# A transformer block stack in split fp32: one more chunk of the feed-forward nets by seven block products, with partial sums kept in PSUM

## The chip, the cores and the metric

The kernel runs on one core of a Trainium2 chip. A core has TensorE (PE, matmuls; its weight loads are listed apart as PEld), VectorE (DVE), ScalarE (ACT), GpSimd (POOL) and SyncE (SP), each with its own row of instructions, and 16 DMA engines. The metric is the time of one execution on the device in microseconds (us), as the median of several runs; a profile of one execution shows what each engine did.

## The reference

Two layers, each of four parts with a layer norm behind each: a feed-forward net `ffn1`, a mixer, cross attention, and a second feed-forward net `ffn2`. The sequence has 256 tokens, the model is 1024 wide, the nets are 2816 wide inside. All of it is fp32.

```python
def swiglu(x, w_gate, w_up, w_down):
    return (jax.nn.silu(x @ w_gate) * (x @ w_up)) @ w_down
...
    for l in range(DEPTH):
        h = layer_norm(ALPHA * h + 0.5 * swiglu(h, ffn1_gate[l], ffn1_up[l], ffn1_down[l]), ln_g[l, 0], ln_b[l, 0])
        ...  # mixer (convolution, recurrence, pooling) and cross attention, each with its layer norm
        h = layer_norm(ALPHA * h + 0.5 * swiglu(h, ffn2_gate[l], ffn2_up[l], ffn2_down[l]), ln_g[l, 3], ln_b[l, 3])
```

The change is in the four nets (`swiglu`) alone.

## The kernel before

**A product is three matmuls.** Each fp32 operand is split in two parts that PE multiplies at its quick fp32 rate: `split` has ACT round a block into `whi` (line 75) and DVE subtract that from the block to give `wlo` (line 76). `mm_rows` then issues hi x hi, hi x lo and lo x hi into one PSUM bank; all its matmuls carry line 132. Every weight of the model is so cast once on ACT and subtracted once on DVE, in pieces of 128x1024. There are eight `whi` and eight `wlo` buffers, used in turn, so ACT and DVE can be at most eight pieces ahead of PE. Blocks come in from DRAM into `raw` buffers (six, in turn) and a few named ones (`spare0` to `spare2`, `lng`, `lnb`) through SP's queue.

**A net.** `ffn` walks over the 2816 hidden columns in five chunks of 512 (numbers 0 to 4) and one of 256 (number 5). A chunk makes its gate and up products for both tiles of 128 tokens in PSUM banks with the tag `acc` (four in turn), applies silu and the product of the two (`activate`, `gated`), turns the result by DMAs and DVE transposes (`turn`, the tiles `dealt` and `square`), splits it into `ah` and `al`, and leaves it in `acts`. The down projection adds up in four banks with the tag `dn`; `both(c, u)` is one slab of it: two splits and 24 matmuls, 128x512. `todo` lists eight slabs of chunks 0 to 3, and they are put between the products of later chunks so that PE has work while a chunk is being turned. `later[c]` tells how many stand right after chunk c.

**Two ways to make a chunk.** `hidden` loads gate and up in eight pieces and issues 96 matmuls of 128x512. `by_seven` takes x as 2 token tiles by 2 halves of the depth, and the weights as 2 halves of the depth by (gate, up), and makes the 2 by 2 block product with seven block products in place of eight: 7 x 12 = 84 matmuls. The sums of blocks of x (`bx`) are made once per net after chunk 1; those of the weights are made in each chunk, in place: `parts_of(r, plus)` adds one block to another on DVE (line 702) and splits the sum, and `more` (line 738) has POOL issue a DMA that adds a block from DRAM into one that has been loaded by `block` (line 685) and used. Which buffers a chunk's blocks live in goes round by `homes`. The first and last blocks are

```python
w00 = block(gate, 0, pieces(*homes[0]))
w01 = block(up, 0, pieces(*homes[1]))
w10 = block(gate, 1, pieces(*homes[3]))
```

and `w11` is loaded after the third product. The seven products are combined partly in PSUM (`run(..., True)` adds to a bank that already holds something) and partly in SBUF: `taken` (line 734) is ACT's copy of a bank, `put` (line 721) is one DVE operation on a bank and an SBUF half. `s` (`sg`) is the gate half, `e` and `f` are the two token tiles of the up half (`halves`, in chunk 5 all of them are in `both`). The tail of a chunk is handed out as functions: `left()` applies the last silu and the last put, what it returns multiplies gate and up (`gate_all`, line 779) and starts the turn, and what that returns ends the turn. So the caller can have the next chunk's instructions written ahead of a tail.

`sevens = (2, 4) if early is not None else (2, 4, 5)` says which chunks go that way; `early` is set in the first net of the program only. So "the last three nets" are ffn2 of layer 0, ffn1 of layer 1 and ffn2 of layer 1; below they are nets 2, 3 and 4. Chunk 5 in them is a half-wide `by_seven` with one piece per block.

**What sets the order.** The tile framework orders the instructions of each engine as they are written, apart from groups under `issue_after`, which are held until a named instruction has been written out, and it puts in the semaphores. Each engine then works off its own row in that order. So an instruction that waits holds up everything behind it on its engine.

## Time and profile before

| | before |
|---|---|
| time, median of 3 runs | 1062.99 us (1062.97 to 1064.28) |
| span of the profiled execution | 1061.1 us |
| PE busy | 1051.2 us, 99%, 6014 matmuls |
| DVE busy | 933.2 us, 88%, 1246 instructions |
| ACT busy | 662.0 us, 62%, 909 |
| POOL busy | 94.7 us, 9%, 128 |
| granted PE clock | 9 tenths or more in all 40 slices |
| moved by DMA | 251.06 MB, mean 237 GB/s |

The span is from the first to the last instruction of one execution that was recorded; no other time of that execution is given, and the median of the timed runs lies 1.9 us above its span. Busy times overlap between engines. PE's matmuls are pipelined, so its duration per matmul (some 0.38 us for 128x512) is longer than the step from one to the next. "L76" is line 76 of the kernel. In a timeline row, the bracket at the end is the idle time of the engine just before the group and what ended it. The chain is the work that ended last, followed back from the end.

### The profile page before, as it was taken

The page shows a single profiled execution, that of the slowest core. Times are in us where ns is not written, and L with a number is a line of the kernel's source. Part 1 is how long each engine was busy: PE and PEld are TensorE (multiplying, and loading weights), DVE is VectorE, ACT ScalarE, POOL GpSimd, SP SyncE. Part 2 cuts the span into 40 slices and gives each one's busy share as a digit, 9 for nine tenths or more (in the row PEclk, how much of TensorE's full clock was granted, in tenths as well). Part 3 has the DMA queues.
Part 4 walks back from the last instruction along what each step waited for, and adds up shares of the span by engine and source line. Part 5 has one row for each costly group of instructions (what it writes and reads, how often), then busy time and mean ns, then how long its engine had stood idle before and what let it go on. Part 6 is the DMA issues. An engine that isn't in the chain of part 4 may idle for free.

```text
span 1061.1 us, 16496 instructions
## 1 busy us (share of the span) xinstructions
PE 1051.2 (99%) x6014; PEld 934.8 (88%) x6014; DVE 933.2 (88%) x1246; ACT 662.0 (62%) x909; POOL 94.7 (9%) x128
## 2 busy tenths in 40 slices
PE   9999999999999999999999999999999999999996
PEld 7888888889899888889888888998998998888896
DVE  6998898989988789887898987999899787898787
ACT  6675775676557566655665656666774655675661
POOL 8002001000000001010001001010000000000001
PEclk9999999999999999999999999999999999999999
DMA  9999984854675589988789978866636675799971
GB/s 364 296 320 280 260 272 146 268 166 155 210 271 179 171 281 231 363 192 217 239 305 254 338 224 208 271 233 222 206 122 215 241 243 162 242 303 294 241 194 68
DMA packets 142306, 251.06 MB, mean 237 GB/s; under 512 B 11249, under 2 KB 51985, under 8 KB 142225
## 3 DMA queue, kind: packets, MB, share of 16 engines
q1 hardware_dynamic: 130656, 228.89, 65.0%
q0 software_dynamic: 10992, 19.94, 10.9%
q10 hardware_dynamic: 576, 1.18, 0.3%
q8 instruction: 47, 0.77, 0.3%
q14 instruction: 35, 0.28, 0.1%
HBM read 234.50 MB, written 1.05 MB: 222 GB/s over the span
## 4 chain that ended last, share of the span: by engine, by line
PE 92%; DVE 3%; DMA 2%; issue 2%; ACT 1%; POOL 0%; DVEq 0%; ACTq 0%; POOLq 0%
PE acc L132 61%; PE dn L132 27%; DVE wlo L76 2%; PE acc L199 1%; DMA raw<-in_ffn_gate_dram 1%; DMA raw<-in_ffn_down_dram 1%; ACT whi L75 0%; PE dn L1139 0%; DVE raw L702 0%; PE dn L1213 0%; DMA lng<-in_ln_g_dram 0%; DMA h<-in_x_dram 0%; DVE al L76 0%; PE acc L581 0%; DVE square L531 0%
## 5 line engine op out<-in xcount | busy, mean ns | idle before, releaser
L75 ACT CAST whi<-raw 128x1024 fp32r<-128x1024 f32 (+1 forms) x452 | 456.1, 1042 | 201.2 <-PE dn L132 58.0
L76 DVE TENSOR_TENSOR wlo<-raw,whi 128x1024 fp32r<-128x1024 f32 (+1 forms) x452 | 534.5, 1211 | 53.1 <-ACT whi L75 47.1
L132 PE MATMUL acc<-whi,xT 128*128 128x512 f32 (+1 forms) x1064 | 313.9, 372 | 0.0
L132 PEld LDWEIGHTS acc<-whi,xT 128*128 128x128 f32 x1064 | 199.0, 189 | 26.9 <-DVE xT L76 0.3
L132 PE MATMUL acc<-wlo,xT 128*128 128x512 f32 (+1 forms) x532 | 197.9, 372 | 0.0
L132 PE MATMUL dn<-whi,ah 128*128 128x512 f32 x346 | 131.5, 380 | 0.0
L132 PE MATMUL dn<-wlo,ah 128*128 128x512 f32 x346 | 131.3, 379 | 0.0
L132 PE MATMUL dn<-whi,al 128*128 128x512 f32 x346 | 131.1, 379 | 0.0
L132 PE MATMUL acc<-xT,whi 128*128 128x512 f32 x480 | 117.6, 381 | 0.0
L132 PEld LDWEIGHTS acc<-wlo,xT 128*128 128x128 f32 x532 | 100.6, 189 | 13.4
L132 PEld LDWEIGHTS acc<-xT,whi 128*128 128x128 f32 x480 | 86.8, 190 | 9.8
L132 PE MATMUL dn<-whi,xT 128*128 128x512 f32 x288 | 87.7, 380 | 0.0
L132 PEld LDWEIGHTS dn<-wlo,ah 128*128 128x128 f32 x346 | 65.4, 189 | 9.6 <-DVE wlo L76 0.6
L132 PEld LDWEIGHTS dn<-whi,al 128*128 128x128 f32 x346 | 65.4, 189 | 9.2
L132 PEld LDWEIGHTS dn<-whi,ah 128*128 128x128 f32 x346 | 65.4, 189 | 9.0
L132 PEld LDWEIGHTS acc<-xT,wlo 128*128 128x128 f32 x480 | 62.9, 191 | 3.2
L132 PE MATMUL acc<-xT,wlo 128*128 128x256 f32 x480 | 63.2, 275 | 0.0
L132 PE MATMUL acc<-wlo,kTh 128*128 128x512 f32 (+1 forms) x176 | 61.7, 351 | 0.0
L132 PE MATMUL acc<-whi,kTl 128*128 128x512 f32 (+1 forms) x176 | 61.7, 351 | 0.0
L132 PE MATMUL acc<-whi,kTh 128*128 128x512 f32 (+1 forms) x176 | 61.7, 351 | 0.0
L132 PEld LDWEIGHTS dn<-whi,xT 128*128 128x128 f32 x288 | 54.4, 189 | 7.6
L132 PE MATMUL dn<-wlo,xT 128*128 128x512 f32 x144 | 54.6, 379 | 0.0
(252 smaller groups left out, 1296.8 us busy)
## 6 DMA issues: line engine op xcount, KB each, us to landing
raw<-in_ffn_up_dram SPq DMA_DIRECT2D x88, 512.0 KB, 5.7
raw<-in_ffn_down_dram SPq DMA_DIRECT2D x88, 512.0 KB, 5.6
raw<-in_ffn_gate_dram SPq DMA_DIRECT2D x84, 512.0 KB, 5.6
raw<-in_w_in_dram SPq DMA_DIRECT2D x48, 512.0 KB, 4.8
dealt<-sg SPq DMA_DIRECT2D x80, 128.0 KB, 4.5
raw<-in_ffn_up_dram POOLq DMA_DIRECT2D x19, 512.0 KB, 6.3
raw<-in_ffn_gate_dram POOLq DMA_DIRECT2D x16, 512.0 KB, 9.4
raw<-in_ca_k_dram SPq DMA_DIRECT2D x16, 512.0 KB, 5.2
```

The lines of the kernel that those rows point to most:

```text
L75: rounded = nc.scalar.copy(hi, src)
L76: lows.append(nc.vector.tensor_tensor(lo, src, hi.bitcast(F32), op=ALU.subtract))
L132: turns.append(nc.tensor.matmul(o, w, x, start=start, stop=stop, skip_group_check=more))
L199: turns.append(nc.tensor.transpose(pt[:, k, :], src[:, (4 * j + k) * P : (4 * j + k + 1) * P], unit))
```

## The change

In the last three nets `sevens` becomes (2, 3, 4, 5): chunk 3 is made by seven block products as well, and the two slabs that stood behind chunk 3 (`later[3] = 2`; the 2 for chunk 5 was not used) go between the products of chunk 3, as `between[0]` and `between[1]`, as chunks 2 and 4 have them. Chunks 2 to 5 then follow each other by seven. Since chunk 3 now takes a place in `sevens`, the tuple of `homes` goes on by one for chunk 4.

In all four nets the sums of the seven products are kept in PSUM for longer. The bank of the first product, `o`, is copied to a second bank, `total`, by ACT, and the third product adds into `o`, which silu then reads directly; products 4, 5 and 7 add into `total`, and after the fourth ACT writes `-total` into a fourth bank, `less`, to which product 6 adds. That takes away two `put` per chunk (one for `s`, one for `e`) and the copy of `f`. The `put` for `f` now reads `total` itself, before product 7 adds to it.

Last, `left()` is called through to the turn at once in every chunk but chunk 4 (before: in every chunk whose successor is not in `sevens`).

```diff
@@ -718,7 +718,7 @@
                         mm_rows(o, x[0][:, k, :], x[1][:, k, :], wh, wl, k == 0 and not more, k == 3, more)
 
                 def put(o, a, op, b):
-                    nc.vector.tensor_tensor(ordered(o), in_order(a), ordered(b), op=op)
+                    nc.vector.tensor_tensor(ordered(o), ordered(a), in_order(b), op=op)
 
                 if ncol == CHUNK:
                     s, ef = activations(), fp.tile([P, NT, CHUNK], F32, tag="up", name="halves", bufs=1)
@@ -737,43 +737,39 @@
                     for i, x in enumerate(to):
                         nc.gpsimd.dma_start(x, part_of(m, j, i), accum_op=ALU.add)
 
-                o = [bank() for _ in range(3)]
-                run(o[0], part_of_x(0, 0), parts_of(w00))
-                taken(s[:, 0, :], o[0])
-                run(o[1], bx[0], parts_of(w00, w01))
+                o, total, one = (bank() for _ in range(3))
+                run(o, part_of_x(0, 0), parts_of(w00))
+                nc.scalar.copy(total, o)
+                run(one, bx[0], parts_of(w00, w01))
+                taken(e, one)
                 more(w01, up, 1)
-                run(o[2], part_of_x(0, 1), parts_of(w10))
+                run(o, part_of_x(0, 1), parts_of(w10), True)
                 between[0]()
-                put(s[:, 0, :], o[2], ALU.add, s[:, 0, :])
+                activate(s, 0, o)
                 w11 = block(up, 1, pieces(*homes[2]))
-                run(o[0], bx[1], parts_of(w00, w11), True)
+                run(total, bx[1], parts_of(w00, w11), True)
                 if ncol == CHUNK:
                     more(w00, gate, 1)
-                copied = taken(e, o[0])
+                less = bank()
+                copied = nc.scalar.mul(less, total, -1.0)
                 between[1]()
-                nc.scalar.activation(s[:, 0, :], s[:, 0, :], AF.Silu)
-                put(e, o[1], ALU.subtract, e)
                 if ncol == CHUNK:
-                    run(o[0], bx[2], parts_of(w01), True)
-                    taken(f, o[0])
-                    o.append(bank())
-                    run(o[3], bx[3], parts_of(w11))
-                    put(f, o[1], ALU.subtract, f)
-                    run(o[0], part_of_x(1, 1), parts_of(w00), True)
+                    run(total, bx[2], parts_of(w01), True)
+                    put(f, e, ALU.subtract, total)
+                    run(less, bx[3], parts_of(w11), True)
+                    run(total, part_of_x(1, 1), parts_of(w00), True)
                 else:
-                    o.append(bank())
-                    run(o[3], bx[3], parts_of(w11))
-                    run(o[0], bx[2], parts_of(w01), True)
-                    taken(f, o[0])
-                    put(f, o[1], ALU.subtract, f)
+                    run(less, bx[3], parts_of(w11), True)
+                    run(total, bx[2], parts_of(w01), True)
+                    put(f, e, ALU.subtract, total)
                     with tc.issue_after(copied.ins):
                         w = parts_of(w00, w10)
                     between[2]()
-                    run(o[0], part_of_x(1, 1), w, True)
+                    run(total, part_of_x(1, 1), w, True)
 
                 def left():
-                    act = activate(s, 1, o[0])
-                    put(e, o[3], ALU.add, e)
+                    act = activate(s, 1, total)
+                    put(e, e, ALU.add, less)
 
                     def gate_all():
                         passed.append((act, nc.vector.tensor_tensor(s, s, ef, op=ALU.mult)))
@@ -818,7 +814,7 @@
                 return w, ah[:, 2 * u : 2 * u + 2, :], al[:, 2 * u : 2 * u + 2, :]
 
 
-            sevens = (2, 4) if early is not None else (2, 4, 5)
+            sevens = (2, 4) if early is not None else (2, 3, 4, 5)
             passed, dealts, turn_memory = [], [], None
             bx = []
 
@@ -845,7 +841,7 @@
                             rows_of(a, i, k, m, c == u == k == 0, apart)
 
             todo = [(c, u) for c in range(4) for u in range(2)]
-            later = (0, 0, 0, 2, 0, 2) if early is None else (0, 1, 0, 1, 0, 2)
+            later = (0, 0, 0, 0, 0, 0) if early is None else (0, 1, 0, 1, 0, 2)
             for c, (c0, ncol) in enumerate(chunks):
                 if not c:
                     acts.append(first()())
@@ -881,7 +877,7 @@
                         held = []
                         with tc.issue_after(lows[-1].ins):
                             acts[4] = acts[4](held)
-                    acts.append(left() if c + 1 in sevens else left()() if c == 5 else left()()())
+                    acts.append(left() if c == 4 and 5 in sevens else left()() if c == 5 else left()()())
                     if ncol < CHUNK:
                         with tc.issue_after(passed[-1][0].ins), tc.issue_after(passed[-1][1].ins):
                             held[0]()
```

The next rows are those of DVE at the boundary from chunk 2 to chunk 3 in net 2. Before, raw_4211 and raw_4212 are chunk 2's w00 with the second gate block added, raw_4476 and the raw tiles behind it are chunk 3's plain gate pieces, and halves_4224 is chunk 2's `ef`.

```order
L76 TENSOR_TENSOR wlo_4441<-raw_4211,whi_4440 128x1024
L76 TENSOR_TENSOR wlo_4445<-raw_4212,whi_4444 128x1024
L76 TENSOR_TENSOR wlo_4481<-raw_4476,whi_4480 128x1024
L76 TENSOR_TENSOR wlo_4485<-raw_4477,whi_4484 128x1024
L76 TENSOR_TENSOR wlo_4493<-raw_4488,whi_4492 128x1024
L721 TENSOR_TENSOR halves_4224<-acc_4226,halves_4224 128x512
L76 TENSOR_TENSOR wlo_4497<-raw_4489,whi_4496 128x1024
L76 TENSOR_TENSOR wlo_4557<-raw_4552,whi_4556 128x1024
L721 TENSOR_TENSOR halves_4224<-acc_4418,halves_4224 128x512
L76 TENSOR_TENSOR wlo_4561<-raw_4553,whi_4560 128x1024
```

After, on the same engine at the same place; raw_4207 and raw_4208 are that block of chunk 2, raw_4469 and raw_4470 chunk 3's w00, raw_4473 and raw_4474 its w01, halves_4220 is chunk 2's `ef`, acc_4222 is `total`, acc_4355 is `less`.

```order
L76 TENSOR_TENSOR wlo_4435<-raw_4207,whi_4434 128x1024
L76 TENSOR_TENSOR wlo_4439<-raw_4208,whi_4438 128x1024
L76 TENSOR_TENSOR wlo_4487<-raw_4469,whi_4486 128x1024
L702 TENSOR_TENSOR raw_4469<-raw_4469,raw_4473 128x1024
L76 TENSOR_TENSOR wlo_4491<-raw_4470,whi_4490 128x1024
L721 TENSOR_TENSOR halves_4220<-halves_4220,acc_4222 128x512
L76 TENSOR_TENSOR wlo_4509<-raw_4469,whi_4508 128x1024
L702 TENSOR_TENSOR raw_4470<-raw_4470,raw_4474 128x1024
L721 TENSOR_TENSOR halves_4220<-halves_4220,acc_4355 128x512
L702 TENSOR_TENSOR raw_4469<-raw_4469,raw_4589 128x1024
```

Chunk 3's first splits are now followed by the sums of its blocks (L702), each made from the tile that was just split, and chunk 2's put for `f` stands behind the first two splits of chunk 3, with the adds between.

The second place is DVE in chunk 4 of net 2, from the splits of the fourth product's block, after which POOL's adding DMA for the same block is issued, to the splits for the seventh product, which read what that DMA brought. Before (raw_4712 and raw_4713 are w00; sg_4724 and halves_4725 are the gate half and `ef`):

```order
L76 TENSOR_TENSOR wlo_4837<-raw_4712,whi_4836 128x1024
L76 TENSOR_TENSOR wlo_4842<-raw_4713,whi_4841 128x1024
L76 TENSOR_TENSOR wlo_4865<-raw_4860,whi_4864 128x1024
L76 TENSOR_TENSOR wlo_4869<-raw_4861,whi_4868 128x1024
L76 TENSOR_TENSOR wlo_4899<-raw_4716,whi_4898 128x1024
L721 TENSOR_TENSOR sg_4724<-acc_4728,sg_4724 128x512
L76 TENSOR_TENSOR wlo_4903<-raw_4717,whi_4902 128x1024
L76 TENSOR_TENSOR wlo_4921<-raw_4831,whi_4920 128x1024
L76 TENSOR_TENSOR wlo_4925<-raw_4832,whi_4924 128x1024
L76 TENSOR_TENSOR wlo_4942<-raw_4712,whi_4941 128x1024
L721 TENSOR_TENSOR halves_4725<-acc_4727,halves_4725 128x512
L76 TENSOR_TENSOR wlo_4946<-raw_4713,whi_4945 128x1024
```

After (raw_4731 and raw_4732 are w00, square_4726 and al_4725 the turn of chunk 3):

```order
L76 TENSOR_TENSOR wlo_4857<-raw_4731,whi_4856 128x1024
L76 TENSOR_TENSOR wlo_4862<-raw_4732,whi_4861 128x1024
L531 STREAM_TRANSPOSE square_4726<-dealt_4719 128x4x4x32 x2
L76 TENSOR_TENSOR wlo_4886<-raw_4881,whi_4885 128x1024
L76 TENSOR_TENSOR wlo_4890<-raw_4882,whi_4889 128x1024
L76 TENSOR_TENSOR al_4725<-square_4726,ah_4724 128x1024
L76 TENSOR_TENSOR wlo_4918<-raw_4735,whi_4917 128x1024
L76 TENSOR_TENSOR wlo_4922<-raw_4736,whi_4921 128x1024
L76 TENSOR_TENSOR wlo_4939<-raw_4851,whi_4938 128x1024
L76 TENSOR_TENSOR wlo_4943<-raw_4852,whi_4942 128x1024
L76 TENSOR_TENSOR wlo_4959<-raw_4731,whi_4958 128x1024
L76 TENSOR_TENSOR wlo_4963<-raw_4732,whi_4962 128x1024
```

The two puts have gone from between, and chunk 3's two transposes and its `al` split have come in; the splits of the slab's pieces, of w01 and of w11 stand there in both.

The third place is POOL's row of adding DMAs from chunk 2 to chunk 5 of net 2. Before, with raw_4211, raw_4212 of chunk 2, raw_4712 to raw_4717 of chunk 4 and raw_4965 of chunk 5:

```order
L738 DMA raw_4211<-in_ffn2_gate_dram 128x2x512
L738 DMA raw_4212<-in_ffn2_gate_dram 128x2x512
L738 DMA raw_4716<-in_ffn2_up_dram 128x2x512
L738 DMA raw_4717<-in_ffn2_up_dram 128x2x512
L738 DMA raw_4712<-in_ffn2_gate_dram 128x2x512
L738 DMA raw_4713<-in_ffn2_gate_dram 128x2x512
L738 DMA raw_4965<-in_ffn2_up_dram 128x4x256
```

After:

```order
L738 DMA raw_4207<-in_ffn2_gate_dram 128x2x512
L738 DMA raw_4208<-in_ffn2_gate_dram 128x2x512
L738 DMA raw_4473<-in_ffn2_up_dram 128x2x512
L738 DMA raw_4474<-in_ffn2_up_dram 128x2x512
L738 DMA raw_4469<-in_ffn2_gate_dram 128x2x512
L738 DMA raw_4470<-in_ffn2_gate_dram 128x2x512
L738 DMA raw_4735<-in_ffn2_up_dram 128x2x512
L738 DMA raw_4736<-in_ffn2_up_dram 128x2x512
L738 DMA raw_4731<-in_ffn2_gate_dram 128x2x512
L738 DMA raw_4732<-in_ffn2_gate_dram 128x2x512
L738 DMA raw_4982<-in_ffn2_up_dram 128x4x256
```

Four adding DMAs of 512 KB have come in for chunk 3, between those of chunk 2 and chunk 4.

## The prediction

> **What bounds the kernel now.** I read the page first, then the chain of waits, the stretches of the three nets that change, and the timeline of DVE inside the second net (ffn2 of layer 0). The page and its groups:

> ```profile
> PE 1051.2 (99%) x6014; PEld 934.8 (88%) x6014; DVE 933.2 (88%) x1246; ACT 662.0 (62%) x909; POOL 94.7 (9%) x128
> PE 92%; DVE 3%; DMA 2%; issue 2%; ACT 1%; POOL 0%; DVEq 0%; ACTq 0%; POOLq 0%
> ```

> TensorE (PE) is busy throughout and is 92% of the chain. But VectorE (DVE) has only 12% of the span left, and the chain of waits shows what happens at the end of the second net:

> ```profile
> 372.79 41.44 PE acc L132 x192
> ...
> 519.21 1.15 DVE wlo L76
> ...
> 520.40 7.17 PE dn L132 x32
> ```

> While PE runs alone, 192 matmuls start in 41.44 us, 0.216 us each. At 520.40 the chain comes to PE out of a DVE split: there PE's next weights were late. The stretches from the first split of chunk 2 to the last down weights, one row for each of the last three nets:

> ```profile
> 390.30:520.30 130.00, 130.00 (x643) 114.57 (x641) 113.54 (x116) 80.69 (x92) 12.35 (x11) 1.00 0.89 255
> 557.50:687.50 130.00, 130.00 (x645) 115.00 (x644) 114.78 (x116) 81.09 (x92) 12.36 (x11) 1.00 0.88 257
> 913.00:1044.00 131.00, 131.00 (x650) 115.87 (x649) 114.64 (x118) 79.40 (x90) 12.33 (x11) 1.00 0.84 240
> ```

> Columns are length, then busy time of PE, weight loads, DVE, ACT, POOL, then the granted clock (1.00). DVE's idle time is 16.5, 15.2 and 16.4 us. This is the budget on which the change draws. Most of it came in 14 gaps:

> ```profile
> DVE wlo L76 <- ACT whi L75: 11.2, 10, 2.0
> DVE al L76 <- ACT ah L75: 3.0, 2, 2.4
> DVE square L531 <- DMA dealt<-sg: 1.6, 2, 0.8
> ```

> **The change part by part.** First, what an instruction costs on DVE when it follows another without a gap, from its timeline:

> ```profile
> 394.04 1.31 DVE L531 STREAM_TRANSPOSE square<-dealt 128x512 f32<-128x512 f32 x2 [0.78 <-DMA dealt<-sg]
> 397.70 1.23 DVE L76 TENSOR_TENSOR al<-square,ah 128x1024 fp32r<-128x1024 f32 x1 [2.36 <-ACT ah L75]
> ...
> 411.51 1.22 DVE L702 TENSOR_TENSOR raw<-raw 128x1024 f32<-128x1024 f32 x1
> 413.92 2.36 DVE L76 TENSOR_TENSOR wlo<-raw,whi 128x1024 fp32r<-128x1024 f32 x2 [1.19 <-ACT whi L75]
> ...
> 468.18 6.89 DVE L76 TENSOR_TENSOR wlo<-raw,whi 128x1024 fp32r<-128x1024 f32 x6
> ...
> 493.57 0.68 DVE L721 TENSOR_TENSOR halves<-acc,halves 128x512 f32<-128x512 f32 x1
> 494.17 2.35 DVE L76 TENSOR_TENSOR wlo<-raw,whi 128x1024 fp32r<-128x1024 f32 x2
> ...
> 499.99 0.42 DVE L721 TENSOR_TENSOR both<-acc,both 128x256 f32<-128x256 f32 x1
> 500.32 2.35 DVE L76 TENSOR_TENSOR wlo<-raw,whi 128x1024 fp32r<-128x1024 f32 x2
> ```

> Six 128x1024 splits take 6.89 us, the last one 1.22, so one follows another after (6.89 - 1.22) / 5 = 1.135 us; after a gap it costs 1.22, 0.085 more. The 512-wide one costs 494.17 - 493.57 = 0.60, the 256-wide one 0.33.

> *PE.* Chunk 3 goes from 96 matmuls to 7 x 12 = 84: 12 x 0.216 = 2.6 us less in each of three nets, 7.8 in all. This is the floor: nothing else leaves PE.

> *DVE.* Chunk 3 splits 7 blocks of two pieces instead of 8 pieces (+6), adds +4 block sums (w00+w01, then +w11, two pieces each), and one 128x1024 gate product: 11 x 1.135 = 12.5 us. Its two 512-wide products with PSUM become two put's: 0. The seeded banks take away two put's in chunks 2 and 4 (4 x 0.60) and two in the half chunk 5 (2 x 0.33): -3.1. Sum +9.4 us per net. In the first net only the four put's go (-2.4 us of DVE), in a net that PE sets: 0.

> [...]

> *ACT.* It takes 6 casts more, and as many evictions as before in a seven chunk (5). Its 80.7 us busy in 130 become about 87: hidden, and the cover is large. The seed of total (after product 1, needed by product 4) has products 2, 3 and a slab, 48 x 0.216 = 10.4 us, as cover; the seed of less has a slab and product 5, 7.8 us. If that cover went, each would cost PE some 0.6 us.

> *The new wait.* put(f) now reads the bank that product 7 adds to, so PE's seventh product waits for a DVE instruction (before: for an ACT copy). In DVE's row that put stands behind the next chunk's first splits, so product 7 also waits for the next chunk's first load. Cover: product 6, 2.6 us, and DVE's lead. I price it within DVE's sum: while DVE is the later engine, it is the same lateness.

> *What of the 9.4 fits.* DVE's lost time before is 16.5 + 14 x 0.085 = 17.7 us. If DVE binds to the end of the net, the net changes by 9.4 + (lost time after) - 17.7. Lost time after: (a) the three gaps of the rows above (0.78, 2.36, 1.19) lie ahead of the first moved instruction and stay: 4.3 + 0.3 = 4.6. (b) An add that is followed at once by the split of its own sum costs 1.19 (the row at 413.92: add, cast on ACT, split). The order after has this once more in chunk 3 (raw_4470), once in chunk 5, and once in chunk 5 with a put between: 2 x 1.27 + (1.27 - 0.60) = 3.2. That makes 7.8, and -0.5 for the second net; with the idle budgets of the others +0.7 and -0.4. Sum -0.2 us, if no DMA is late.

> (c) The DMAs that add a block into one already loaded (line 738, `more`). POOL's timeline, where the gate pair of chunk 4 is issued; ACT's, where the cast waits for it; the landings of the whole second net up to 520; and the page's issues, plain (SPq) and adding (POOLq):

> ```profile
> 470.84 2.42 POOL L738 DMA_DIRECT2D raw<-in_ffn_gate_dram  x2 [14.75 <-DVE wlo L76]
> ```

> ```profile
> 481.15 1.05 ACT L75 CAST whi<-raw 128x1024 fp32r<-128x1024 f32 x1 [1.03 <-DMA raw<-in_ffn_gate_dram]
> ...
> 484.81 2.00 ACT L75 CAST whi<-raw 128x1024 fp32r<-128x1024 f32 x2 [2.13 <-DMA raw<-in_ffn_gate_dram]
> ```

> ```profile
> L738 POOL DMA_DIRECT2D raw<-in_ffn_up_dram x5: 1189/1194/1295, 393.6 to 489.8; - x5
> L738 POOL DMA_DIRECT2D raw<-in_ffn_gate_dram x4: 1189/1192/1281, 411.9 to 472.0; - x4
> ...
> DMA to landing us min/median/max: 5.9/9.5/12.8
> ```

> ```profile
> raw<-in_ffn_gate_dram SPq DMA_DIRECT2D x84, 512.0 KB, 5.6
> ...
> raw<-in_ffn_up_dram POOLq DMA_DIRECT2D x19, 512.0 KB, 6.3
> raw<-in_ffn_gate_dram POOLq DMA_DIRECT2D x16, 512.0 KB, 9.4
> ```

> The adding DMAs rise from 9 to 13 per net. Each gate one is issued after the fourth product's split and has to be back before the seventh's. In chunk 4 after the change, 8 big instructions and two transposes lie between on DVE: 8 x 1.135 + 1.3 = 10.4 us, less the cast's 1.05: 9.3. The pair issued at 470.84 landed in time for the casts at 481.15, 10.3 us on, and at 484.81, 12.8 us after the second issue (ACT waited 1.03 and 2.13 for them): 1.0 to 3.5 us of lost time, 0 at the shortest landing. I take 1.0, near the first of the pair, since fewer SP loads run beside it. Chunk 3 has the same cover at the median landing, 0.2; its first load, which may start only after chunk 2's fifth product is split, has 7 instructions (7.9 - 1.05 = 6.9 us) against 5.6: 0, or 2.5 if it is as slow as 9.4. I take 0.4 for both. So (c) is 1.4 per net, between 0 and 7.0.

> Sum: -0.2 + 3 x 1.4 = +4.0 us. The page's execution has a span of 1061.1 us; the median of the runs, 1062.99, lies 1.9 above it, and I carry that over: 1061.1 + 4.0 + 1.9 = 1067.0 us.

> **The rivals.** (1) PE stays the bound and the change gains. The point is 17.7 - 9.4 = 8.3 us of lost time per net: below it the kernel is faster, at 5.7 the full 7.8 us come (1055.2). For it: many casts waited only because DVE was ahead and the ring of eight whi buffers was full:

> ```profile
> L75 ACT CAST whi<-raw 128x1024 fp32r<-128x1024 f32 (+1 forms) x452 | 456.1, 1042 | 201.2 <-PE dn L132 58.0
> ```

> and such waits go when the lead goes. Against it: (a) and (b) alone are 7.8 and are none of this kind, which leaves 0.5 for everything else. But (a) and (b) are taken from single rows, and a third off them already decides it. Chance 0.28.

> (2) No DMA is late: the adding DMAs land as the fast ones here do (5.9), the cover of 9.3 suffices, and gain and cost cancel: 1061.1 - 0.2 + 1.9 = 1062.8. For it: the up ones land after 6.3 at the median. Against: the gate ones took 9.4. Chance 0.25. [...]

> (3) The close pair in chunk 4 lands as late as 12.8 in each net: 3.5 + 0.4 = 3.9 per net, +11.5: 1074.5. For it: the trace has it so in the second net, and more adding DMAs share the queues. Chance 0.14.

> **How the numbers follow.** The forecast (1 to 2 us of late DMA per net, slower by 0.4%) has the remaining 0.33. A measurement of this kernel tells about 0.2%, 2.1 us, from no change. Faster is rival 1: 0.28; the same is rival 2: 0.25; slower are the forecast and rival 3: 0.47. The range goes from 1057.7 (rival 1 with two thirds of its gain, 1063.0 - 5.3; some 0.12 below) to 1074.5 (rival 3 in every net; some 0.07 above).

> **What the new profile would show.** If the steps hold: DVE's busy time in the three stretches rises by 8 to 9 us and its idle falls to about 9 to 10; PE shows waits that it hardly had before, for wlo (L76) late in chunks 4 and 5 and for halves (L721) ahead of seventh products, 2.5 to 5 us per net; chunk 3 on PE is 18.1 us long plus its slabs. The first net keeps its length. Wrong would be: no PE wait over 1 us in these nets (rival 1); waits of DVE for casts that wait for a DMA of 3 us and more (rival 3); or a wait of PE for ACT's seeds, which I price at 0.

## The result and the profile after

The kernel after takes 1078.07 us (median of 4 runs, 1075.05 to 1078.72) against 1063.63 for the kernel before in the same runs: a ratio of 1.0129 [1.0116, 1.0141], 14.4 us slower. The sign was the forecast one; the size, 4.0 us, was far off, and the time lies above the range. The profiled execution after has a span of 1076.5 us and took 1078.4, so it too has 1.9 us around its span.

From the page after, the lines on the engines, on the chain by engine, and the two adding DMA groups:

```profile
PE 1050.8 (98%) x5978; PEld 930.9 (86%) x5978; DVE 956.7 (89%) x1257; ACT 680.4 (63%) x936; POOL 110.0 (10%) x140
...
PE 70%; issue 12%; DMA 8%; DVE 7%; ACT 2%; POOL 1%; DVEq 0%; POOLq 0%; SPq 0%; ACTq 0%
...
raw<-in_ffn_up_dram POOLq DMA_DIRECT2D x25, 512.0 KB, 6.3
raw<-in_ffn_gate_dram POOLq DMA_DIRECT2D x22, 512.0 KB, 9.1
```

36 matmuls have gone, as worked out, and DVE's busy time has grown by 23.5 us. But the chain was 92% PE and is now 70%; DMA and DVE have 15% of it, and the adding DMAs are no slower at the median (9.1 us, before 9.4). What PE waits for in the changed kernel (total us, number of waits, longest; before, its list has two waits, both ahead of the first net):

```profile
PE acc L132 <- DVE halves L721: 13.5, 4, 4.5
PE dn L132 <- ACT whi L75: 2.2, 3, 1.3
...
PE acc L132 <- ACT whi L75: 0.4, 1, 0.4
PE acc L132 <- DVE wlo L76: 0.2, 1, 0.2
```

Four waits carry most of it, and three of the four are one place: the first matmul of product 7 in chunk 4, once in each of the three nets. PE's timeline:

```profile
494.71 0.45 PE L132 MATMUL acc<-whi,xT 128*128 128x512 f32 x1 [3.56 <-DVE halves L721]
...
664.93 0.77 PE L132 MATMUL acc<-whi,xT 128*128 128x512 f32 x1 [4.52 <-DVE halves L721]
...
1029.30 0.76 PE L132 MATMUL acc<-whi,xT 128*128 128x512 f32 x1 [4.01 <-DVE halves L721]
```

Measured from the start of one matmul to the next, these stalls are 3.72, 4.68 and 4.17 us beyond the usual step: 12.6 us. The second and third cost more than their wait. The windows around the second (PE, weight loads, DVE, ACT, POOL, granted clock, DMA share, GB/s), and last the one behind the first stall:

```profile
660.00:665.00 5.00, 0.48 (x3) 0.11 (x2) 4.18 (x4) 2.21 (x3) 0.52 (x1) 0.87 0.74 270
665.00:670.00 5.00, 5.00 (x12) 4.00 (x13) 4.65 (x5) 3.16 (x4) 0.77 (x1) 0.50 0.73 105
...
495.00:500.00 5.00, 5.00 (x35) 4.67 (x34) 4.87 (x5) 3.80 (x6) 0.57 (x1) 1.00 0.80 127
```

Behind the stall of 4.68 us the granted clock is 0.50, and PE issues 12 matmuls in 5 us where 23 would fit; that cost 2.7 us, and 1.5 behind the one of 4.17. Behind 3.72 the clock stayed at 1.00; the last section says what tells the cases apart. Adding up all steps between matmuls that were longer than usual, the three nets waited 1.8, 0.6 and 0.6 us before and 7.1, 9.0 and 10.6 after: +23.7, less the 7.8 of the removed matmuls, is +15.9; the spans differ by 15.4. So the stall and its slow clock at this one place are 16.8 us, and the rest is many waits of 0.4 to 1.6 us, some of which stood before.

**What lies behind the wait.** In net 3, chunk 4, after the change: the row of POOL that issues the adding gate pair (`more`), PE's first matmul of product 4, ACT's cast that waits for the pair, and DVE from there to the put:

```profile
646.78 2.42 POOL L738 DMA_DIRECT2D raw<-in_ffn_gate_dram  x2 [10.19 <-DVE wlo L76]
...
647.26 0.38 PE L132 MATMUL acc<-whi,kTh 128*128 128x512 f32 x1
...
659.49 1.99 ACT L75 CAST whi<-raw 128x1024 fp32r<-128x1024 f32 x2 [3.86 <-DMA raw<-in_ffn_gate_dram]
...
660.57 2.36 DVE L76 TENSOR_TENSOR wlo<-raw,whi 128x1024 fp32r<-128x1024 f32 x2 [2.68 <-ACT whi L75]
662.96 1.22 DVE L702 TENSOR_TENSOR raw<-raw 128x1024 f32<-128x1024 f32 x1
664.10 0.68 DVE L721 TENSOR_TENSOR halves<-halves,acc 128x512 f32<-128x512 f32 x1
```

And the same place before (POOL; PE's first matmul of product 4 and of product 7; the first cast that waits for the pair; the copy of `f` that freed the bank then):

```profile
637.73 2.41 POOL L738 DMA_DIRECT2D raw<-in_ffn_gate_dram  x2 [14.75 <-DVE wlo L76]
...
645.71 0.38 PE L132 MATMUL acc<-whi,kTh 128*128 128x512 f32 x1
...
658.66 0.38 PE L132 MATMUL acc<-whi,xT 128*128 128x512 f32 x1
...
650.68 1.05 ACT L75 CAST whi<-raw 128x1024 fp32r<-128x1024 f32 x1 [1.59 <-DMA raw<-in_ffn_gate_dram]
...
657.07 0.58 ACT L734 COPY halves<-acc 128x512 f32<-128x512 f32 x1
```

The chain from POOL's first issue is nearly the same length in both: after, 646.78 (issue) to 659.49 (the second of the pair has landed) is 12.7 us, and through cast, split, the next chunk's first split and sum and the put to product 7 it is 664.93 - 646.78 = 18.2. Before, the second landed in time for the cast 12.95 us after the first issue, and the copy ended at 657.65, 19.9 after the issue (0.7 of it a wait of ACT for PE). Counted from its own issue, the second DMA of the pair took 10.8, 11.5 and 11.0 us in the three nets, and 12.8, 11.7 and 12.4 before: it came no later. What changed is how far PE was behind when the pair was issued. PE has 60 matmuls to do from product 4 to product 7 (products 4, 5, 6 and a slab), 12.95 us, which is 658.66 - 645.71 before. Product 4 started 8.0 us after the issue before, and 0.5 after it now. So the room was 20.9 us for a chain of 19.9, and is 13.4 for one of 18.2. In the three nets DVE's lead at product 4 (from the end of a split to the first matmul that reads it) was 8.5 to 8.65 us before and is 1.0 to 1.35 now.

### The profile page after: what moved, and what is told of

Read it like the earlier page. It is cut to its first block, busy times and chain, and to the rows that moved or that the text cites. A ratio compares the mean times of both kernels' runs of the same rounds, so it can differ in the third digit from the quotient of the medians.

```text
span 1076.5 us, 16511 instructions
## 1 busy us (share of the span) xinstructions
PE 1050.8 (98%) x5978; PEld 930.9 (86%) x5978; DVE 956.7 (89%) x1257; ACT 680.4 (63%) x936; POOL 110.0 (10%) x140
## 3 DMA queue, kind: packets, MB, share of 16 engines
HBM read 240.80 MB, written 1.05 MB: 225 GB/s over the span
## 4 chain that ended last, share of the span: by engine, by line
PE 70%; issue 12%; DMA 8%; DVE 7%; ACT 2%; POOL 1%; DVEq 0%; POOLq 0%; SPq 0%; ACTq 0%
PE acc L132 44%; PE dn L132 23%; DMA raw<-in_ffn_gate_dram 6%; DVE wlo L76 3%; ACT whi L75 2%; DMA raw<-in_ffn_up_dram 2%; DVE raw L702 1%; PE acc L199 1%; POOL raw L738 1%; DVE halves L721 0%; PE dn L1135 0%; DMA raw<-in_ffn_down_dram 0%; DVE h L407 0%; DMA h<-in_x_dram 0%; PE dn L1209 0%
## 5 line engine op out<-in xcount | busy, mean ns | idle before, releaser
L76 DVE TENSOR_TENSOR wlo<-raw,whi 128x1024 fp32r<-128x1024 f32 (+1 forms) x470 | 552.0, 1208 | 47.6 <-ACT whi L75 42.8
L75 ACT CAST whi<-raw 128x1024 fp32r<-128x1024 f32 (+1 forms) x470 | 471.1, 1041 | 187.5 <-DVE raw L702 75.2
L132 PE MATMUL acc<-whi,xT 128*128 128x512 f32 (+1 forms) x944 | 282.2, 376 | 13.8 <-DVE halves L721 13.5
L132 PEld LDWEIGHTS acc<-whi,xT 128*128 128x128 f32 x944 | 178.4, 191 | 39.9 <-issue 13.2
L132 PE MATMUL acc<-wlo,xT 128*128 128x512 f32 (+1 forms) x472 | 176.9, 375 | 0.2 <-DVE wlo L76 0.2
L132 PE MATMUL dn<-whi,ah 128*128 128x512 f32 x346 | 130.3, 381 | 2.2 <-ACT whi L75 2.2
L132 PE MATMUL dn<-wlo,ah 128*128 128x512 f32 x346 | 131.2, 379 | 0.0
L132 PE MATMUL dn<-whi,al 128*128 128x512 f32 x346 | 131.1, 379 | 0.0
L132 PE MATMUL acc<-xT,whi 128*128 128x512 f32 x480 | 117.6, 381 | 0.0
L132 PEld LDWEIGHTS acc<-wlo,xT 128*128 128x128 f32 x472 | 90.5, 192 | 12.6 <-DVE wlo L76 0.6
L132 PEld LDWEIGHTS acc<-xT,whi 128*128 128x128 f32 x480 | 86.8, 190 | 9.8
L132 PE MATMUL dn<-whi,xT 128*128 128x512 f32 x288 | 87.7, 380 | 0.0
L132 PE MATMUL acc<-whi,kTh 128*128 128x512 f32 (+1 forms) x224 | 80.2, 358 | 0.0
L132 PE MATMUL acc<-wlo,kTh 128*128 128x512 f32 (+1 forms) x224 | 79.9, 357 | 0.0
L132 PE MATMUL acc<-whi,kTl 128*128 128x512 f32 (+1 forms) x224 | 79.9, 357 | 0.0
L132 PEld LDWEIGHTS dn<-whi,ah 128*128 128x128 f32 x346 | 65.2, 189 | 12.1 <-ACT whi L75 3.4
L132 PEld LDWEIGHTS dn<-whi,al 128*128 128x128 f32 x346 | 65.4, 189 | 9.2
L132 PEld LDWEIGHTS dn<-wlo,ah 128*128 128x128 f32 x346 | 65.4, 189 | 9.1 <-DVE wlo L76 0.3
L132 PEld LDWEIGHTS acc<-xT,wlo 128*128 128x128 f32 x480 | 62.9, 191 | 3.2
L702 DVE TENSOR_TENSOR raw<-raw 128x1024 f32<-128x1024 f32 x53 | 63.8, 1216 | 0.2
L132 PE MATMUL acc<-xT,wlo 128*128 128x256 f32 x480 | 63.2, 275 | 0.0
L132 PEld LDWEIGHTS dn<-whi,xT 128*128 128x128 f32 x288 | 54.4, 189 | 7.5
## 6 DMA issues: line engine op xcount, KB each, us to landing
raw<-in_ffn_up_dram SPq DMA_DIRECT2D x88, 512.0 KB, 6.1
raw<-in_ffn_down_dram SPq DMA_DIRECT2D x88, 512.0 KB, 5.9
raw<-in_ffn_gate_dram SPq DMA_DIRECT2D x84, 512.0 KB, 6.0
raw<-in_w_in_dram SPq DMA_DIRECT2D x48, 512.0 KB, 4.7
raw<-in_ffn_up_dram POOLq DMA_DIRECT2D x25, 512.0 KB, 6.3
raw<-in_ffn_gate_dram POOLq DMA_DIRECT2D x22, 512.0 KB, 9.1
raw<-in_ca_k_dram SPq DMA_DIRECT2D x16, 512.0 KB, 5.1
```

What stands on the lines that cost most here:

```text
L75: rounded = nc.scalar.copy(hi, src)
L76: lows.append(nc.vector.tensor_tensor(lo, src, hi.bitcast(F32), op=ALU.subtract))
L132: turns.append(nc.tensor.matmul(o, w, x, start=start, stop=stop, skip_group_check=more))
L702: nc.vector.tensor_tensor(r[i], r[i], plus[i], op=ALU.add)
```

## The experiments

The names of the theories in the expectations: BUDGET, DVE has too much to do in these nets; ROW, product 7 waits for what stands ahead of put(f) in DVE's row, late loads and splits of the next chunk; LANDING, the late adding DMA pair of chunk 4 is what holds that row up. The reading given above, called LOOP, was formed only after the first fifteen runs had refuted parts of each: a closed chain (issue, landing, cast, split, the next chunk's first split and sum, put) against PE's work in between plus DVE's lead. Diffs are against the kernel after unless said otherwise, and show the lines that matter; `...` stands for what is left out. All measured times (medians), with the kernel before in the same runs and the ratio with its 95% interval:

| run | us | before | ratio |
|---|---|---|---|
| e1_act_copies_f | 1076.36 | 1063.78 | 1.0114 [1.0088, 1.0141] |
| e2_no_late_add | 1066.39 | 1063.78 | 1.0025 [1.0015, 1.0034] |
| e3_seeded_alone | 1064.16 | 1063.78 | 1.0001 [0.9992, 1.001] |
| e4_chunk3_unseeded | 1082.85 | 1063.78 | 1.0172 [1.0156, 1.0187] |
| e5_no_sums_c3 | 1087.89 | 1063.77 | 1.0227 [1.021, 1.0244] |
| e6a_put_first_all | 1098.74 | 1063.77 | 1.0328 [1.0312, 1.0343] |
| e6b_put_first_c4 | 1072.83 | 1063.77 | 1.0079 [1.0063, 1.0094] |
| e7_next_ahead | 1076.27 | 1063.77 | 1.0129 [1.0098, 1.016] |
| e8a_put_between | 1078.63 | 1063.49 | 1.0147 [1.0129, 1.0166] |
| e8b_put_between_c4 | 1074.99 | 1063.49 | 1.0108 [1.0086, 1.013] |
| e10_sums_on_pool | 1104.23 | 1063.49 | 1.0366 [1.034, 1.0393] |
| e12_between_no_late_add | 1073.04 | 1063.49 | 1.0088 [1.0072, 1.0103] |
| e13_short_sums_c3 | 1075.86 | 1063.36 | 1.011 [1.0091, 1.013] |
| e14_short_sums_no_late_add | 1067.17 | 1063.36 | 1.0032 [1.0019, 1.0045] |
| e15_extra_dve | 1070.16 | 1063.36 | 1.007 [1.0055, 1.0085] |
| e16_both_slabs_c4 | 1066.18 | 1063.64 | 1.0023 [1.0014, 1.0033] |
| e17_both_slabs_c34 | 1064.99 | 1063.64 | 1.0016 [1.0006, 1.0025] |
| e18_half_slab | 1073.14 | 1063.5 | 1.0094 [1.0077, 1.0111] |

### The two halves of the change

Seeded banks alone, chunk 3 as before:

```diff
-            sevens = (2, 4) if early is not None else (2, 3, 4, 5)
+            sevens = (2, 4) if early is not None else (2, 4, 5)
...
-            later = (0, 0, 0, 0, 0, 0) if early is None else (0, 1, 0, 1, 0, 2)
+            later = (0, 0, 0, 2, 0, 2) if early is None else (0, 1, 0, 1, 0, 2)
...
-                    acts.append(left() if c == 4 and 5 in sevens else left()() if c == 5 else left()()())
+                    acts.append(left() if c + 1 in sevens else left()() if c == 5 else left()()())
```

> The seeded banks without chunk 3: chunk 3 is made of 96 matmuls as before, with its two slabs behind it. PE has as many matmuls as before, DVE 3.1 us less in each of three nets. ROW with the lead lost to chunk 3: the put of f stands in the same place of DVE's row as in the changed kernel, but DVE still has its lead, and PE comes to chunk 4's seventh product late enough: no stall over 0.5 us, 1063.6 (within 2). If the put in that place is enough by itself, without chunk 3: stalls of 2 to 4 us in chunk 4 of each net, 1072. BUDGET: 1063, the same as before, since PE bounds it there.

Chunk 3 by seven in the kernel before, that is the reverse of the three edits above made there, without seeded banks:

> Chunk 3 by seven with the sums made as before (ACT copies, four more DVE operations in each seven chunk): DVE has 12.5 us more per net than before, not 9.4. BUDGET: worse than the changed kernel by up to 3 x 3.1, 1087. ROW: no product waits for a put; seventh products wait for ACT copies behind two casts; DVE, whose lead in chunk 4 is 0.1 to 0.5 us in the changed kernel, is late there by some 3 us per net; 7.8 are saved on PE: 1063.6 - 7.8 + 3 x (3 + 1.5) = 1069, with a slow clock perhaps 1073. LANDING: 1078.

The seeds alone change nothing that can be measured. With chunk 3 by seven they are worth 1082.85 - 1078.07 = 4.8 us. In e4 PE waits for splits (L76) above all, 7.4 us in 14 waits, where the seeds have taken puts out of DVE's row. All of the loss comes from chunk 3.

### What product 7 waits for

Two edits take away one link each: ACT copies `f`, so that put(f) frees no bank any more (the same two lines also stand in for the put of the half-wide chunk 5); and chunk 4 leaves out the late adding pair in the last three nets (its seventh product then lacks the second gate block).

```diff
-                    put(f, e, ALU.subtract, total)
+                    taken(f, total)
+                    nc.vector.tensor_tensor(f, e, f, op=ALU.subtract)
...
```

> ACT copies the bank total into f after the fifth product, as before, and DVE subtracts in SBUF, so the seventh product no longer waits for a DVE instruction. DVE's work is the same. Three theories. ROW: the seventh product waits for the put of f, which stands in DVE's row behind the split of a late block, a split and an add of the next chunk. The copy stands in ACT's row behind two casts only, so the stalls of 3.7, 4.7 and 4.2 us in chunk 4 fall to 1.1, 1.9 and 1.4, and the slow clock behind two of them (4.2 us in all) goes: 1078.1 - 8.2 - 4.2 = 1066. BUDGET (the prediction's): DVE simply has too much to do; its work is unchanged, so 1078. LANDING: the late adding DMA alone sets the stall; it is as late as ever, so about 1075.

```diff
-                if ncol == CHUNK:
+                if ncol == CHUNK and (early is not None or c0 != 4 * CHUNK):
                     more(w00, gate, 1)
```

> In the last three nets chunk 4 leaves out the DMA that adds the second gate block (its seventh product uses a wrong block); everything else as after. ROW: DVE's gaps of 1.9, 2.7 and 2.2 us go, but the put of f still stands behind three instructions of 1.135 us, so chunk 4 still stalls for 1.6 to 1.8 us in each net, now too short for the slow clock: 1078.1 - 7.4 - 4.2 = 1066.5. LANDING: the stalls of chunk 4 go altogether: 1078.1 - 12.6 - 4.2 = 1061.3. BUDGET: DVE's work is the same and the stall turns up elsewhere: 1076 or more.

PE's waits, first with ACT's copy, then without the late pair:

```profile
PE dn L132 <- ACT whi L75: 6.1, 5, 1.5
PE acc L132 <- ACT halves L734: 4.0, 4, 1.9
PE acc L132 <- DVE wlo L76: 2.8, 4, 0.9
PE acc L132 <- ACT both L734: 2.1, 3, 0.7
```

```profile
PE acc L132 <- DVE halves L721: 6.0, 5, 1.8
PE dn L132 <- ACT whi L75: 2.2, 3, 1.3
```

Without the pair 11.7 us of the 14.4 are gone; the stalls shrink to 1.8 to 1.9 and no slow clock is left (granted clock 1.00 in the stretches of all three nets). With ACT's copy the stall at product 7 fell about as foreseen (0.35, 1.65, 2.05 us; a stretch of half clock still followed the last), but the time came back: as waits for casts and splits elsewhere, and as 2.1 us for the added copy in chunk 5 (`both`). The total missed its expectation by 10 us. In this kernel a shorter wait at one place was not worth its length.

### Moving the put

If put(f) were only in the wrong place in DVE's row, moving it should cure it. `issue_after` holds back the splits of product 7 until put(f) has been written, in every 512-wide chunk (e6a) or in chunk 4 alone (`and c0 == 4 * CHUNK`, e6b):

```diff
-                    put(f, e, ALU.subtract, total)
+                    done = put(f, e, ALU.subtract, total)
                     run(less, bx[3], parts_of(w11), True)
-                    run(total, part_of_x(1, 1), parts_of(w00), True)
+                    with ExitStack() as behind:
+                        if early is None:
+                            behind.enter_context(tc.issue_after(done.ins))
+                        w = parts_of(w00)
+                    run(total, part_of_x(1, 1), w, True)
```

> In every seven chunk of 512 of the last three nets the put of f is written out ahead of the splits for the seventh product, so on DVE it stands ahead of them and of the next chunk's. ROW: the waits of seventh products for it go (14.1 us and the slow clock, 4.2). But DVE now waits for PE's fifth and sixth product at each such place and enters the next chunk with no lead: the sum of its first block is split 2.3 us late, at 3 places in 3 nets, which gives back some 15 to 20: 1078 again, with waits for wlo in place of halves. BUDGET: the same 1078 with the waits of before; the kind of wait tells them apart. If the order costs nothing: 1060.

> The same order in chunk 4 alone, where DVE waits for the late DMA anyhow. ROW: the put of f starts as soon as product 5 is done, the seventh product starts on its first piece and waits 0 to 0.5 us for the second; no slow clock. Chunk 5 then takes back some of it, about 2 us a net: 1078.1 - 12.6 - 4.2 + 6 = 1067. LANDING: the late block comes no earlier, so 1.9 to 2.7 us per net stay: 1068 to 1070. BUDGET: 1078.

Later in the row: put(f) between product 7's splits and the next chunk's, in chunk 4 between the two splits; in all chunks (e8a), or in chunk 4 alone (e8b, which adds `and ncol < CHUNK` to the first condition). e12 is e8b without the late pair.

```diff
+                        with ExitStack() as then:
+                            if behind is not None and i >= behind[1]:
+                                then.enter_context(tc.issue_after(behind[0].ins))
+                            split(h, w, r[i])
...
+                run(o, part_of_x(0, 0), parts_of(w00, None, (dones[-1], 0) if dones and early is None else None))
...
+                    dones.append(put(f, e, ALU.subtract, total))
...
+                    run(total, part_of_x(1, 1), parts_of(w00, None, (dones[-1], 1) if early is None and c0 == 4 * CHUNK else None), True)
```

> The put of f stands on DVE between the splits of the seventh product and those of the next chunk (in chunk 4 between the two splits of the seventh product); the put of e is not moved ahead as it was in the run that cost 35 us. ROW: no seventh product waits over 0.5 us; DVE waits for PE's fifth product at each such put, with work for 5.2 us of PE split ahead, so chunks 3 and 4 begin with a lead of about 1 us and PE waits little: 1066 to 1071. If any order that makes DVE wait for PE costs as much as it saves: 1078 or more.

> The same in chunk 4 alone. Near the earlier run with the put first in chunk 4 (1072.8), since DVE is the later engine there in both: ROW 1071, with waits of PE for splits (wlo) spread over chunks 4 and 5, 6 to 7 us per net less the 2.6 saved. LANDING: 1068.

> As the second run here, and chunk 4 of the last three nets leaves out its adding gate DMA (the seventh product uses a wrong block). ROW: with the put in its place the late DMA has little left to hold up (DVE waits for PE or for the DMA at about the same time): 1069. LANDING: it is worth the 11.7 us that it was worth in the kernel as changed: 1060.

What DVE waits for with the put first everywhere (e6a), and what PE waits for in that kernel:

```profile
DVE halves L721 <- PE acc L132: 17.3, 7, 5.6
```

```profile
PE acc L132 <- DVE wlo L76: 10.9, 6, 1.8
PE acc L132 <- ACT whi L75: 10.2, 18, 0.9
```

The waits at product 7 are gone, but put(f) needs PE's fifth product, and while DVE stands still for it (17.3 us) its lead is used up: PE then waits for splits and casts everywhere. The misses grow with the number of chunks touched: e6a 20.7 us over its expectation, e6b 5.8. The place further back did no better: e8a is level with the change, 7.6 us above the top of what was expected, and e8b is 4.0 above. In e12 the late pair is worth only about 2 us (e8b less e12; the runs of e8b spread over 5), where with the put as the change has it it was worth 11.7: the pair costs what it does through the put behind it. But moving the put costs 6.65 against e2 (1073.04 - 1066.39). That is not DVE waiting for PE at the put, for which e12 shows no wait; the first splits and the sum of chunk 5 now stand behind it, ACT's casts come later (DVE waits 25.1 us for them, in e2 18.1), and PE waits for casts and splits in chunk 5.

Placing the next chunk's first product ahead of product 7 on PE (the function becomes a generator that yields after product 1, and chunks 2 to 4 each start the next one) gave 1076.27: the put was only moved three places further back on DVE, and in the profiled execution, which took 1082.49 and was the slowest of four, PE waited 12.5 us in six places for L721.

> The first product of the next chunk is put ahead of the seventh of this one on PE, so that PE has 2.6 us of other work (1.3 us ahead of chunk 5, which is half as wide) while DVE comes to the put of f and the late block lands. The work of DVE and the DMAs is the same. ROW: chunk 4's stalls fall by 1.3 us each, the one of 1.6 us in chunk 2 goes, and the slow clock goes: 1078.1 - 3.9 - 1.6 - 4.2 = 1068. BUDGET: 1078. LANDING: 1074.

### Is it the amount of DVE's work?

Three edits take DVE's sums in chunk 3 away: all of them (e5; chunk 3's products then use blocks that are not summed), by shortening each to 32 of 512 columns so that the waits stay (e13), and that without the late pair (e14).

```diff
-                        if plus is not None:
+                        if plus is not None and c0 != 3 * CHUNK:
```

> Chunk 3 of the last three nets leaves out its four block sums on DVE (its products use unsummed blocks), so DVE has 4 x 1.135 = 4.5 us less per net ahead of chunk 4; rows, DMAs and PE are else as after. If DVE's lead is what chunk 3 used up (the prediction's budget, seen as a lead): chunk 4's adding DMAs start 4.5 us earlier against PE, the stalls of 3.7, 4.7 and 4.2 us and the slow clock go: 1078.1 - 12.6 - 4.2 = 1061. If the place of the put in DVE's row or the landing after 11 us is enough by itself, whatever DVE's lead: 1078.

```diff
+                            cols = slice(0, 32 if c0 == 3 * CHUNK else ncol)
+                            nc.vector.tensor_tensor(r[i][:, :, cols], r[i][:, :, cols], plus[i][:, :, cols], op=ALU.add)
```

> As the changed kernel, but the four block sums of chunk 3 on DVE work on a sixteenth of their columns (32 of 512; its products use blocks that are mostly unsummed). All instructions, waits and DMA orders stay; DVE has some 4 x 1.0 = 4 us less per net. If DVE's work is what is paid (BUDGET): 1078.1 - 3 x 4 = 1066, and with the lead that it wins chunk 4's stalls shrink too, down to 1058. If the put's place and late blocks alone are paid (ROW), a DVE that is further ahead meets loads that are not there yet, as in the run without sums (1087.9): 1076 or more.

> The same, and chunk 4 leaves out its adding gate DMA too. Without short sums that run gave 1066.4, with stalls of 1.8 to 1.9 us left before chunk 4's seventh product. BUDGET: DVE's work is what is left, so 1066.4 - 3 x 2 = 1060 (below before). ROW: the put still stands behind three instructions, but DVE comes to them 4 us earlier: also 1060 or less. If both are wrong and PE waits for loads: 1066 or more.

Leaving 4.5 us of DVE's work per net out made it 9.8 us slower. The adding DMAs then waited for no sum: in net 2 chunk 3's up pair was issued at 418.57 and 420.91 us in place of 430.87 and 434.88, beside chunk 3's first gate loads. These took 8.5 to 12.0 us to land in place of 6.6 to 7.5, and put(f) of chunk 2 stood behind them. ACT's and DVE's rows of that kernel at chunk 2 of net 2:

```profile
434.08 4.83 ACT L75 CAST whi<-raw 128x1024 fp32r<-128x1024 f32 x5 [4.54 <-DMA raw<-in_ffn_gate_dram]
...
435.15 2.36 DVE L76 TENSOR_TENSOR wlo<-raw,whi 128x1024 fp32r<-128x1024 f32 x2 [4.36 <-ACT whi L75]
437.43 0.68 DVE L721 TENSOR_TENSOR halves<-halves,acc 128x512 f32<-128x512 f32 x1
```

PE's stalls at chunk 2's product 7 were 4.62, 3.92 and 6.99 us in the three nets. In e13 the lead in chunk 4 came back in part and its stalls went to 0, 1.55 and 1.51, but late loads now stalled chunks 2 and 3 (up to 2.77): about 2 us gained of the 14.4. e14 is no better than e2. So the amount alone does not decide it. The sums on POOL (e8b with `nc.gpsimd` for the fourth product's sums in chunks 2 to 4) cannot tell more: each took 3.2 us on POOL by the profile against 1.22 for the DVE instruction that it replaced, and the run is 29 us slower than e8b:

> As the run before, and in chunks 2, 3 and 4 of the last three nets the two sums of the fourth product's block are made by POOL in place of DVE, with the same reads and writes: 6 x 1.135 = 6.8 us of DVE's work less per net. Once the put no longer stands in a bad place, what is left of the loss (1071 against 1055.2 for PE alone) is DVE's work: by BUDGET the waits for wlo go and the time falls to 1060 or lower, below before. If POOL's adds are slow (an add of 128x1024 takes it more than the 5 us that the fourth product can wait), or slow DVE's beside them: 1071 or more, with waits for POOL.

```profile
L702 POOL TENSOR_TENSOR raw<-raw 128x1024 f32<-128x1024 f32 x18 | 58.2, 3231 | 30.2 <-DVE wlo L76 25.5 <-DMA raw<-in_ffn_down_dram 2.9 <-DMA raw<-in_ffn_up_dram 1.4
```

The other way round: the kernel before with eight additional 128x1024 adds on DVE in chunk 3 of each of the last three nets, 9.1 us of work, and nothing else changed (no seeds, no more DMAs):

```diff
+                def extra():
+                    if early is None and c0 == 3 * CHUNK:
+                        x = fp.tile([P, DM], F32, tag="spare2", name="extra", bufs=1)
+                        nc.vector.tensor_tensor(x, h[0], h[0], op=ALU.add)
...
```

> The kernel before, with eight more DVE instructions of 128x1024 in chunk 3 of each of the last three nets, one behind each split (their results are not used): 8 x 1.135 = 9.1 us more of DVE's work per net, about what the change adds (9.4), and nothing else changed on PE, in DMAs or in the puts. By the prediction's working DVE's lost time before is 17.7 us per net, of which 4.6 stay: 9.1 fits and the time stays at 1063.6 (within 2). If DVE's work alone makes the loss: 1063.6 + 3 x 5 = 1078.

PE's waits in it:

```profile
PE acc L133 <- ACT halves L741: 5.7, 3, 2.8
```

By the prediction's sum it should have cost nothing, since DVE had 16 us to spare per net. It cost 6.8 us. In the profiled execution, the slowest of four at 9.6 us over before, all of it lies at one place: product 7 of chunk 4, three stalls (2.18, 2.94, 1.11 us), and some 3.4 us of half clock behind the first two. DVE's lead there fell from 8.6 to between 4.8 and 6.6, and the old copy of `f` was late by what was missing. DVE's idle time was not free: in chunk 4 all of its lead but about 1 us was already being used by the loop.

### Giving the loop its room

If LOOP is right, work for PE between product 4 and product 7 must cure it, with nothing taken off DVE or the DMAs. Chunk 4's two slabs go both between products 4 and 5 (one stood ahead of product 4); then PE has 84 matmuls there, 18.1 us. e17 does it in chunk 3 too (`c in (3, 4)`).

```diff
+                        [lambda: None, lambda: (both(*todo.pop(0)), both(*todo.pop(0)))] if c == 4 and early is None else
                         [lambda: both(*todo.pop(0))] * 2 if ncol == CHUNK else
```

> The changed kernel, with chunk 4's two slabs both between its fourth and fifth product (before: one ahead of the fourth). DVE's work, the DMAs and the put's place stay. LOOP, the theory as it now stands: from the end of the fourth product's split over POOL's issue, the landing, cast, split, the next chunk's split and add, to the end of the put takes 17 us; PE has 2.6 + 5.2 + 2.6 + 2.6 = 13 us of work there, plus DVE's lead of 1 us; here it has 18.2. So chunk 4's seventh product waits less than 0.5 us and no slow clock follows. The fourth product comes 5.2 us sooner and its splits are 2 to 3 us late: 1078.1 - 12.6 - 4.2 + 3 x 2.5 = 1069. If it is DVE's work that is paid, the wait only moves: 1076 or more.

> The same in chunks 3 and 4. In the changed kernel chunk 3 had no such stall in any net, so nothing is to be won there, and its fourth product waits 2 to 3 us for splits: LOOP 1069 + 3 x 2 = 1075; if more cover for the adding DMA also helps chunk 4 by an earlier start: 1069.

PE's waits, e16 and then e17:

```profile
PE acc L132 <- DVE wlo L76: 2.5, 4, 0.8
PE acc L132 <- ACT whi L75: 2.1, 3, 0.8
```

```profile
PE acc L132 <- DVE wlo L76: 3.8, 7, 0.8
PE acc L132 <- ACT whi L75: 1.9, 3, 0.8
```

One line moved 5.2 us of PE's own work per net and brought 11.9 us back. No wait for `halves` is left in either, with all the sums, adding DMAs and the put where the change has them. In net 3 of e16 the put ends at 659.60 and PE comes to product 7 at 659.87, so the room is just enough. e17 is 1.0016 of before: the whole change then costs about what it saves. What remains are waits of up to 0.8 us each for splits and casts, three and more per net, most of them at product 4, which now comes 5.2 us sooner. e16's expectation of 1069 and e17's of 1069 and 1075 were all too high.

From e17, half a slab back ahead of product 4 in chunks 3 and 4, so that product 4 is not late itself (only half a slab's splits are issued ahead; the rest follows product 4):

> As the run with both slabs behind the fourth product in chunks 3 and 4, but half a slab (12 matmuls, one piece of its weights) goes back ahead of the fourth product. PE gets 2.6 us of work there for 1.135 us of DVE's, so the fourth product's waits (2 us in chunk 4 of each net) fall to about 0.5; the loop keeps 13 + 2.6 = 15.6 us and a lead of 1 against a chain of 17, so the seventh product waits 0 to 0.7. LOOP: 1065.0 - 3 x 1 = 1062 to 1063, level with before or just below it. If the loop must have all of the 18 us: chunk 4's seventh product waits 1 to 2 us again, 1067.

That missed: PE then has 15.5 us (72 matmuls) against a chain of 18.2, and stalled 2.73, 2.41 and 2.59 us, about that difference; the lead of 1 us on which the expectation counted was not there (0.06). No version that was run is faster than before.

## Why the prediction was right in sign and wrong in size

- *PE.* and *DVE.* hold: 36 matmuls fewer, DVE +23.5 us against 3 x 9.4 less 2.4, or 25.8. *ACT.* holds: no matmul waits for the seeds (weight loads waited 1.0 us in four places), and seeds alone change nothing (e3). The first net keeps its length. The waits for halves (L721) ahead of seventh products came where they were forecast; those for splits hardly did (0.2 us). Slower, with 0.47 of the chances, was the likeliest of three outcomes and no more.
- *What of the 9.4 fits* (-0.2 us, or about 0 when it is worked without rounding) agrees with e17, which has room in the loop and is 1.4 us over before. That is agreement in the total and no test of its terms, since e17 also moves where product 4 waits.
- The step that failed is *The new wait.*: "I price it within DVE's sum: while DVE is the later engine, it is the same lateness." It was not the same. PE waits at product 7 for a chain that starts with DVE's own split of product 4, and when that chain is longer than PE's work in between, DVE stands idle in the middle of it (2.68 us ahead of the split at 660.57) while PE waits. Nobody works off anything then.
- With it fell the cover in (c). It was counted along DVE's row from split to split (9.3 us), and a shortfall of 1.0 was the price, taken near the first of the pair. It is the second that holds DVE up: for 1.89, 2.68 and 2.16 us. And the chain that had to be covered was 18.2 us long, with the next chunk's split and sum and the put behind the landing; its cover was PE's 12.95 us plus DVE's lead of 8.0, both readable before. (c) put 1.0 us per net on chunk 4; the runs show 4.2 of stall and 1.4 of slow clock on the mean.
- Rival (3) took the right place but not the right cause. It needed the second of the pair to land as late as 12.8 us after its own issue, and that took 10.8 to 11.5. Its 3.5 us per net is nearer to the stall than (c)'s 1.0 by luck, since it too ended at the split.
- The rows showed that the landing was not new: before, in net 3, the pair also came 12.95 us after its issue. It was hidden by the lead. The prediction counted DVE's idle time as a budget and never asked what the lead was covering; e15 shows that the kernel before already stalls when 9 us of DVE's budget are spent.
- The half clock behind stalls of about 4 us was in none of the cases.
- In stretches of the changed kernel that hold about the same work (391.4 to 523.5, 560.9 to 696.5 and 921.9 to 1059.8 us) DVE's busy time is 8.6, 8.3 and 8.8 us higher, as forecast, but its idle time is 10.0, 12.5 and 14.4 rather than 9 to 10: part of the budget was still there, unused, inside the waits.

Open: why e1's waits came back in so many other places, and why e13's loads were late in chunks 2 and 3 when only the length of the sums was changed.

## What to carry to other kernels

When an instruction frees a buffer or starts a load that comes back to the same engine, write down the whole loop (issue, landing, cast, split, everything queued ahead of the last link) and compare it with the consumer's work in between plus the producer's lead; idle time of the producer is not a budget while its lead covers such a loop. An edit that takes work off the bound engine and gives some to the next one can shorten that cover, as the lead went from 8 us to 1 here. The cheap cure in this kernel was order: filler work of the consumer inside the loop, not ahead of it (e16, 11.9 us by one line).

## What the runs showed of the hardware

```profile
489.60:493.01 3.41, 1.55 (x8) 1.02 (x6) 2.63 (x3) 1.67 (x2) 0.00 (x0) 1.00 0.92 327
493.01:496.42 3.41, 1.71 (x8) 1.55 (x9) 2.84 (x4) 2.36 (x3) 1.29 (x1) 1.00 0.56 184
660.26:663.67 3.41, 0.14 (x1) 0.00 (x0) 3.07 (x3) 1.22 (x2) 0.00 (x0) 1.00 0.83 294
663.68:667.09 3.41, 2.16 (x5) 1.83 (x6) 2.84 (x5) 2.82 (x3) 1.29 (x1) 0.50 0.37 95
```

```profile
492.51:495.92 3.41, 1.40 (x7) 1.05 (x7) 2.22 (x3) 2.77 (x4) 1.29 (x1) 1.00 0.34 80
495.92:499.33 3.41, 3.41 (x11) 2.78 (x10) 3.41 (x5) 1.80 (x3) 0.00 (x0) 0.50 0.94 143
```

The stall of 3.72 us lay across two intervals and left PE 1.55 and 1.71 us of work in them; the shorter one in e15 left 1.40 in one, and half clock followed. An estimate from all 20 traces: count as idle what the step from one matmul to the next has beyond the usual one. Then all 23 half-clock stretches between the first 21 us and the last product follow an interval with at least 2.13 us of idle time, and no interval at full clock with 2.07 or less was followed by one. After the change such stretches cost 1.5 and 2.7 us on top of the stall.

**An add on POOL.** An add of 128x1024 fp32 took 3.23 us on POOL at the mean (e10; the profile's times on POOL are rough) against 1.22 on DVE, 2.6 times.
